# The opening of a one-core decoder layer, in a written order: loads split and regrouped, block 0 first, four weight tiles ahead

## The chip, the cores and the metric

The kernel runs on one core of a Trainium2 chip. A core has five engines, each with its own queue of instructions that it works off in order: TensorE (PE in the profile; PEld is its loading of weights), VectorE (DVE), ScalarE (ACT), GpSimd (POOL) and SyncE (SP), which here only issues transfers between main memory and the on-chip memory. Engines wait for each other through semaphores. The metric is the time of one execution on the device in microseconds (us); lower is better.

## The reference

One layer of a decoder on 256 rows (tokens) of 2048 columns in float32. Nine vectors of 2048 (shift, scale and gate for each of three sub-layers) are made from a conditioning vector c; then come a SwiGLU network, a pair of token mixers (retention and windowed attention) side by side, a second SwiGLU network and a last norm. Only the first lines matter here:

```python
c_act = silu(c)
mod = (c_act @ w_ada + b_ada).reshape(b, 9, 2048)
h = rms_norm(x, norm_ffn1) * (1 + mod[:, 1]) + mod[:, 0]
gate, up = split(h @ w_ffn1_gu, 2)            # 2048 x 11264
x = x + 0.5 * mod[:, 2] * ((silu(gate) * up) @ w_ffn1_down)
h = rms_norm(x, norm_mix) * (1 + mod[:, 4]) + mod[:, 3]
...
```

So nothing of the first large product can start before silu(c), two rows of 128 columns of `mod` for the block at hand, and the root mean square of the rows of x are known.

## The kernel before

**Products.** The 256 rows are two row tiles t of 128; the 2048 columns are 16 blocks k of 128. A large product keeps full float32 accuracy with three TensorE products: each operand is split into a high part (a cast to the rounded format on ACT) and a low part (a subtraction on DVE), and high x high, low x high and high x low are added in one PSUM bank (`products`, L327 to L329). `split` (L335 on ACT, L336 on DVE) makes the parts of a weight tile; `modulated` (L497 on ACT, L502 on ACT, L503 on DVE) applies shift and scale to a block of x, already turned so that columns lie on partitions, and makes its two parts `held.hi` and `held.lo` (hh and hl in the profile).

**Conditioning.** One row (m, k) of the transposed `w_ada` is a tile of 128 x 2048 (1 MB). DVE multiplies it with silu(c), which stands in all 128 partitions (`cact`), and sums along the row: a *pass* (`ada_pass`, L204), here two passes of 1024 columns a row. `ada_end` (L221 to L224) adds the two sums, the bias and, for a scale, the gain. silu(c) comes from four TensorE products of a row of ones with a quarter of c (L170), which copies c to all partitions, and four ACT operations (L171).

**The first stage.** Twelve column tiles n of `w_ffn1_gu` (512 columns each; even n gates, odd n ups) go through five groups of blocks k: 0 to 1, 2 to 4, 5 to 7, 8 to 11, 12 to 15. In each group `visit` loads one tile for the group's blocks, splits it and adds its products; the sum is moved from PSUM to on-chip memory by `to_parts` (L837, L835) and added to by the next group. While a group runs, a generator `group` works off the rows (1, k) and (0, k) of the next group, one row at a time between the tiles, and then scales (L787), turns (L788) and modulates the blocks. The first group's rows, blocks and both row tiles' norms come ahead of the loop.

**What sets the order.** SP's queue has the order of the code. On the other engines a planner orders instructions by its own estimates, within the dependencies, except where `manual_schedule(engines=ORDERED)` gives the code's own order to PE, DVE and ACT too; before, that is done around the norms between stages, not in the opening. A weight tile waits for one of four `raw` buffers, a split for one of three buffers (`wsp`), a row of conditioning after the first two for one of two ring places. A transfer of SP also waits until the eighth before it has landed.

**The opening's loads.** In SP's order: c; row (1, 0) in halves; the two row tiles of x (L762); the unit matrix, three norm gains and the biases (L151 to L157); rows (0, 0), (1, 1), (0, 1) in halves; then the weight tiles (L808). `columns_in` (L178 to L188) turns gains and biases with PE and copies them with DVE. The squares of x are summed by ACT, eight operations of 512 columns (L462); `inv_rms` (L474 to L488) makes the inverse root, with one ACT root. GpSimd's queue holds the load of the tables and masks (L879) and of the sinks (L880), at the start, and then the gate rows (L281).

## Time and profile before

| | |
|---|---|
| time, median of three runs | 2431.64 us (2431.32 to 2433.16) |
| profiled execution: its span from the first to the last instruction | 2429.6 us |
| PE busy | 2385.2 us (98%) |
| DVE busy | 1701.3 us (70%) |
| ACT busy | 1236.0 us (51%) |
| mean rate of the transfers | 250 GB/s |
| first product of a weight tile (L327) | at 26.57 us |

The time of the profiled execution itself is given only by its span; the three timed runs lie 1.7 to 3.6 us above it.

Rows of the profile are read like this. In a view in order of time: start, duration, engine, line of the kernel, operation, what it writes and reads, how often, and in brackets the idle time of the engine before it with what ended that. In a view of groups: line, engine, operation, tiles, shapes, count, then busy us and the mean of one in ns, then the idle time in front of the group and what ended it. In a view of windows: the stretch, its length, then for each engine busy time and number of instructions, then the granted clock of TensorE, the busy share of the transfer engines and GB/s. In a view of transfers: tiles, issuing queue, count, KB each, and the us from issue to landing. A matmul's duration covers its way through the pipeline; successive ones start closer together.

### The profile page before, as it was taken

What the parts mean: (1) busy time and instruction counts of PE and PEld (TensorE: products, weight loads), DVE (VectorE), ACT (ScalarE), POOL (GpSimd) and SP (SyncE); (2) the same over time, 40 slices, a digit from 0 to 9 for tenths busy, and PEclk for the clock granted to TensorE, in tenths of its full rate; (3) what the DMA queues carried; (4) which work ended last, traced back from release to release, by engine and by line L of the source; (5) the groups of instructions that cost most, each with busy time, mean ns of one, the idle gap of its engine ahead of it and who ended that gap; (6) DMA issues with size and microseconds to landing.
All of it is one profiled execution on the core that took longest, in us unless ns stands there. A gap on an engine that the chain in (4) does not pass through costs nothing. (4 is left out here: it accounts for less than half of the span.)

```text
span 2429.6 us, 29064 instructions
## 1 busy us (share of the span) xinstructions
PE 2385.2 (98%) x10798; PEld 1946.8 (80%) x10798; DVE 1701.3 (70%) x2735; ACT 1236.0 (51%) x1696; POOL 5.7 (0%) x14
## 2 busy tenths in 40 slices
PE   7999999999999999999999999999999999999998
PEld 4778888888787777788888888887788888888886
DVE  6998777778877677886666776767655555555656
ACT  6544545454545455554544444446554555554544
POOL 0000000000000000000000000000000000000000
PEclk9999999999999999999999999999999999999999
DMA  9987689998875665566676777755677777775563
GB/s 347 341 333 284 217 313 318 356 319 295 311 264 186 243 222 204 206 219 216 233 266 245 251 260 260 279 189 190 215 249 237 243 251 238 248 237 192 185 198 122
DMA packets 274545, 606.43 MB, mean 250 GB/s; under 512 B 40098, under 2 KB 40482, under 8 KB 255586
## 3 DMA queue, kind: packets, MB, share of 16 engines
q1 hardware_dynamic: 272898, 597.91, 70.8%
q0 software_dynamic: 928, 5.61, 0.6%
q8 instruction: 85, 1.39, 0.2%
q10 hardware_dynamic: 576, 1.05, 0.1%
q14 instruction: 58, 0.47, 0.1%
HBM read 595.06 MB, written 2.12 MB: 246 GB/s over the span
## 5 line engine op out<-in xcount | busy, mean ns | idle before, releaser
L336 DVE TENSOR_TENSOR wl<-raw,wh 128x1024 fp32r<-128x1024 f32 (+1 forms) x828 | 995.9, 1208 | 591.2 <-ACT wh L335 585.3
L335 ACT CAST wh<-raw 128x1024 fp32r<-128x1024 f32 (+1 forms) x828 | 861.4, 1042 | 973.0 <-PE pa L328 936.8
L327 PE MATMUL pa<-wh,hh 128*128 128x512 f32 x2224 | 870.5, 393 | 3.4 <-ACT wh L335 2.9
L328 PE MATMUL pa<-wh,hl 128*128 128x512 f32 x2224 | 869.9, 391 | 2.2 <-DVE hl L503 1.8
L329 PE MATMUL pa<-wl,hh 128*128 128x512 f32 x2224 | 798.0, 392 | 4.0 <-DVE wl L336 4.0
L327 PEld LDWEIGHTS pa<-wh,hh 128*128 128x128 f32 x2224 | 418.1, 188 | 93.4 <-ACT wh L335 4.4
L329 PEld LDWEIGHTS pa<-wl,hh 128*128 128x128 f32 x2224 | 415.9, 188 | 95.9 <-DVE wl L336 9.8
L328 PEld LDWEIGHTS pa<-wh,hl 128*128 128x128 f32 x2224 | 418.3, 188 | 89.8 <-DVE hl L503 2.5
L328 PE MATMUL pa<-wh,a 128*128 128x512 f32 x992 | 383.9, 389 | 0.0
L327 PE MATMUL pa<-wh,a 128*128 128x512 f32 x992 | 367.1, 390 | 1.6 <-DVE t L546 1.2
L329 PE MATMUL pa<-wl,a 128*128 128x512 f32 x992 | 367.1, 390 | 0.8 <-DVE wl L336 0.8
L327 PEld LDWEIGHTS pa<-wh,a 128*128 128x128 f32 x992 | 186.1, 188 | 41.5 <-DVE t L546 1.9
L329 PEld LDWEIGHTS pa<-wl,a 128*128 128x128 f32 x992 | 185.9, 188 | 40.6 <-DVE wl L336 2.4
L328 PEld LDWEIGHTS pa<-wh,a 128*128 128x128 f32 x992 | 186.3, 188 | 38.5
L204 DVE CUSTOM_DVE_ANT_0 slot<-slot,cact 128x512 f32<-128x512 f32 (+1 forms) x252 | 192.8, 814 | 10.5 <-DMA slot<-in_w_ada_dram 10.3
L204 DVE CUSTOM_DVE_ANT_0 raw<-raw,cact 128x512 f32<-128x512 f32 (+1 forms) x260 | 167.1, 696 | 42.5 <-DMA raw<-in_w_ada_dram 32.3
L368 DVE TENSOR_TENSOR a<-slot,a 128x512 fp32r<-128x512 f32 x124 | 85.0, 686 | 13.2 <-ACT a L367 13.2
L367 ACT CAST a<-slot 128x512 fp32r<-128x512 f32 x124 | 76.4, 616 | 14.8 <-PE pa L329 14.7
L442 ACT COPY slot<-a 128x512 uint16<-128x512 uint16 x54 | 38.5, 772 | 31.3 <-DMA a<-a 31.3
L204 DVE DVE_READ_ACCUMULATOR2_ANT sums<- 128x1 f32 x512 | 42.4, 83 | 0.0
L418 ACT COPY slot<-ps 128x512 f32<-128x512 f32 x52 | 29.4, 584 | 23.7 <-PE ps L417 23.5
L462 ACT ACTIVATE pd<-x_sb 128x512 f32<-128x512 f32 x32 | 19.0, 593 | 34.6 <-DVE x_sb L547 32.1
(164 smaller groups left out, 1024.2 us busy)
## 6 DMA issues: line engine op xcount, KB each, us to landing
raw<-in_w_ffn_gu_dram SPq DMA_DIRECT2D x152, 1024.0 KB, 5.2
raw<-in_w_in_dram SPq DMA_DIRECT2D x104, 1024.0 KB, 5.0
raw<-in_w_ffn_down_dram SPq DMA_DIRECT2D x88, 1024.0 KB, 5.1
slot<-in_w_ada_dram SPq DMA_DIRECT2D x76, 1024.0 KB, 7.3
raw<-in_w_ada_dram SPq DMA_DIRECT2D x64, 1024.0 KB, 4.8
raw<-in_w_ffn_gu_dram SPq DMA_DIRECT2D x24, 768.0 KB, 6.9
raw<-in_w_swa_branch_dram SPq DMA_DIRECT2D x16, 1024.0 KB, 5.3
raw<-in_w_ret_branch_dram SPq DMA_DIRECT2D x16, 1024.0 KB, 5.1
```

What stands on the lines that cost most here:

```text
L204: nc.vector.tensor_tensor_reduce(out=w[:, at], in0=w[:, at], in1=cact[:, at], scale=1.0, scalar=0.0, op0=ALU.mult, op1=ALU.add, accum_out= ...
L327: nc.tensor.matmul(ps, ah[:, j, ts], wh[:, j, :], start=first, stop=False)
L328: nc.tensor.matmul(ps, al[:, j, ts], wh[:, j, :], start=False, stop=False)
L329: nc.tensor.matmul(ps, ah[:, j, ts], wl[:, j, :], start=False, stop=last)
L335: nc.scalar.copy(hi, src)
L336: nc.vector.tensor_sub(lo, src, hi.bitcast(F32))
L367: nc.scalar.copy(hi, v)
L368: nc.vector.tensor_sub(lo, v, hi.bitcast(F32))
L418: nc.any.tensor_copy(dest, ps[:, : n * P])
L442: nc.any.tensor_copy(into[:, :, :, i], turned[:, i])
L462: nc.scalar.activation(side_bank(), src, AF.Square, accum_out=dest)
```

## The change

- **c.** The first quarter of `cact` is loaded as a broadcast by SP, and silu is done in place; TensorE spreads the other three quarters.
- **Small loads.** The unit matrix, gains and biases are issued by GpSimd. The tables and sinks that stood first in its queue are ordered behind the first gate row's load.
- **x in halves.** Each row tile of x comes in two loads; the second tile of x comes behind row (0, 0) and the first weight tile.
- **Order.** From silu(c) to the products of the first two weight tiles, PE, DVE and ACT follow the code. The first row tile's root is worked out first: two of its four squares on ACT, the other half in one DVE operation of 1024 columns (`far_squares`). Block 0 goes through scaling, turning, modulation and its products for the first row tile, then for the second, then block 1 follows. Weight tiles are split one block at a time. `root_table` loads ACT's root table right behind silu.
- **Fillers.** `warm(n)` puts n plain float32 products (128 x 512) into a bank that nobody reads.
- **Weight tiles ahead.** Tiles 0 to 3 of the first group are loaded during the opening, ahead of the next group's rows. The next group's passes and scalings are ordered behind the opening's last split, and in the first group the rows are drawn behind the fourth to the tenth tile instead of the second to the tenth.

```diff
     def small_loads():
-        nc.sync.dma_start(ident, consts[:, C_ID : C_ID + P])
+        nc.gpsimd.dma_start(ident, consts[:, C_ID : C_ID + P])
         for i, src in enumerate((norm_ffn1, norm_mix, norm_ffn2)):
-            nc.sync.dma_start(
+            nc.gpsimd.dma_start(
...
     cact = one.tile([P, D], F32, tag="cact", name="cact")
-    for j in range(D // CH):
-        pt = acc_bank()
-        nc.tensor.matmul(pt, ones, c_row[:, j * CH : (j + 1) * CH], start=True, stop=True)
-        nc.scalar.activation(cact[:, j * CH : (j + 1) * CH], pt, AF.Silu)
+    nc.sync.dma_start(cact[:, :CH], c[:, :CH].broadcast_to([P, CH]))
+    small_loads()
+
+    def activate_c():
+        for j in range(D // CH):
+            at = slice(j * CH, (j + 1) * CH)
+            src = cact[:, at]
+            if j:
+                src = acc_bank()
+                nc.tensor.matmul(src, ones, c_row[:, at], start=True, stop=True)
+            nc.scalar.activation(cact[:, at], src, AF.Silu)
...
     place(1, 0)
-    for t in range(NT):
-        nc.sync.dma_start(x_sb[:, t, :], x[0, t * P : (t + 1) * P, :])
-    small_loads()
+    x_load(0)
     place(0, 0)
+    first_two = [load_blocks(0, groups[0])]
+    x_load(1)
     place(1, 1)
     place(0, 1)
-    columns_in()
+    first_two.append(load_blocks(1, groups[0]))
...
+                with tc.issue_after(last_split[1] if ks[0] == 2 else opened[1]):
+                    for q in range(passes):
+                        ada_pass(k, rows_of[m, k], early[m], q, passes)
...
+    def far_squares(t):
+        far = x_sb[:, t, D // 2 :]
+        nc.vector.tensor_tensor_reduce(
+            out=junk, in0=far, in1=far, scale=1.0, scalar=0.0,
+            op0=ALU.mult, op1=ALU.add, accum_out=ssq[:, t * 4 + 2 : t * 4 + 3],
+        )
+
+    def warm(n):
+        idle = side_bank()
+        for _ in range(n):
+            nc.tensor.matmul(idle, ident, x_sb[:, 0, :CH], start=True, stop=True)
...
-    for _ in group(groups[0]):
-        pass
+    with tc.manual_schedule(engines=ORDERED):
+        activate_c()
+        root_table()
+        for q in range(passes):
+            first_pass(1, 0, q)
+        loaded[2] = load_blocks(2, groups[0])
+        columns_in()
+        first_end(1, 0)
+        near_squares(0)
+        warm(2)
+        far_squares(0)
+        r.append(inv_rms(ssq, 0, 3))
+        ps = bank()
+        first_turn(ps, 0, 0)
+        for q in range(passes):
+            first_pass(0, 0, q)
+        loaded[3] = load_blocks(3, groups[0])
+        first_end(0, 0)
+        w00 = first_split(0, 0)
+        modulated(held, 0, ps[:, T[0]], 0, act=True, ts=T[0])
+        banks[0] = [acc_bank() for _ in range(NT)]
+        first_products(0, 0, 0, w00)
+        warm(3)
+        near_squares(1, 4)
+        first_pass(1, 1, 0)
+        r.append(inv_rms(ssq, 1))
+        first_turn(ps, 0, 1)
+        first_pass(1, 1, 1)
+        modulated(held, 0, ps[:, T[1]], 0, act=True, ts=T[1])
+        first_products(0, 0, 1, w00)
+        ps = bank()
+        for t in range(NT):
+            first_turn(ps, 1, t)
+        warm(3)
+        for q in range(passes):
+            first_pass(0, 1, q)
+        first_end(1, 1)
+        first_end(0, 1)
+        modulated(held, 1, ps[:, :S], 0, act=True)
+        w01 = first_split(0, 1)
+        for t in range(NT):
+            first_products(0, 1, t, w01)
+        banks[1] = [acc_bank() for _ in range(NT)]
+        w1 = [first_split(1, k) for k in range(2)]
+        for k in range(2):
+            for t in range(NT):
+                first_products(1, k, t, w1[k])
+        opened = list(last_split)
...
-            visit(n, ks, load_blocks(n, ks), n not in stay)
+            if g > 0 or n > 1:
+                raw = loaded.pop(n) if g == 0 and n in loaded else load_blocks(n, ks)
+                visit(n, ks, raw, n not in stay)
             last = len(order) - 2
-            for _ in range((i + 1) * due // last - i * due // last if i < last else i == last):
+            if g == 0:
+                now = max(0, i - 1) * due // (last - 2) - max(0, i - 2) * due // (last - 2)
+            else:
+                now = (i + 1) * due // last - i * due // last
+            for _ in range(now if i < last else i == last):
                 next(coming, None)
...
-    nc.gpsimd.dma_start(small_c[:, C_COS:], consts[:, C_COS:C_DEC])
-    nc.gpsimd.dma_start(sink_b, sinks.broadcast_to([P, QH]))
+    with tc.issue_after(gate_loaded.ins):
+        nc.gpsimd.dma_start(small_c[:, C_COS:], consts[:, C_COS:C_DEC])
+        nc.gpsimd.dma_start(sink_b, sinks.broadcast_to([P, QH]))
```

More of the change, by code (lines that the diff above doesn't have):

```diff
@@ L280, in gate_load @@
     def gate_load(row, m):
-        nc.gpsimd.dma_start(row, gate_d[m // 3][None, :].broadcast_to([P, D]))
+        return nc.gpsimd.dma_start(row, gate_d[m // 3][None, :].broadcast_to([P, D]))
     pace = {"steps": iter(()), "rate": 0.0, "due": 0.0, "behind": None}
@@ new lines, in layer_kernel, with first_pass, first_end, near_squares @@
+    ssq = small(NT * 4, "ssq")
+    r = []
+    junk = part[2][:, 3 * NT * CH :]
+    def first_pass(m, k, q):
+        ada_pass(k, rows_of[m, k], early[m], q, passes)
+    def first_end(m, k):
+        ada_end(m, slice(k, k + 1), early[m], 0 if m else None, passes)
+    def near_squares(t, n=2):
+        for ci in range(n):
+            square_sum(
+                ssq[:, t * 4 + ci : t * 4 + ci + 1], x_sb[:, t, ci * CH : (ci + 1) * CH]
+            )
+    def far_squares(t):
+        far = x_sb[:, t, D // 2 :]
+        nc.vector.tensor_tensor_reduce(
+            out=junk,
+            in0=far,
+            in1=far,
+            scale=1.0,
+            scalar=0.0,
+            op0=ALU.mult,
+            op1=ALU.add,
+            accum_out=ssq[:, t * 4 + 2 : t * 4 + 3],
+        )
@@ L814, in visit, with first_split @@
+    def first_split(n, k):
+        return split(wsp, "w", first_two[n][:, k : k + 1, :], CH)
+    banks, moved = {}, set()
+    chunks = list(range(2 * EARLY))
     def visit(n, ks, raw, ends, step=2):
```

100 lines of the change are left out of this document (54 added, 46 removed).

## The prediction, made before the changed kernel was run

> **What bounds the kernel now.** I read the page first, then windows up to 226 us, then the order of time in the opening, then the groups by form, then the DMA issues.
>
> ```profile
> span 2429.6 us, 29064 instructions
> PE 2385.2 (98%) x10798; PEld 1946.8 (80%) x10798; DVE 1701.3 (70%) x2735; ACT 1236.0 (51%) x1696; POOL 5.7 (0%) x14
> ```
>
> TensorE (PE) bounds the whole, and only the opening and the stage behind it leave it idle. The windows (us of the stretch, then busy time and count of PE, PEld, DVE, ACT, POOL, then clock, DMA share, GB/s):
>
> ```profile
> 12.00:32.32 20.32, 8.43 (x22) 5.81 (x23) 16.56 (x48) 13.14 (x31) 0.00 (x0) 1.00 0.99 367
> 32.32:58.52 26.20, 25.09 (x109) 19.78 (x107) 21.58 (x34) 18.29 (x28) 0.00 (x0) 1.00 1.00 370
> 58.52:160.00 101.48, 97.24 (x418) 76.03 (x418) 94.16 (x146) 49.18 (x75) 0.00 (x0) 1.00 0.87 324
> 160.00:226.00 66.00, 65.59 (x293) 53.93 (x293) 62.48 (x95) 32.27 (x45) 0.00 (x0) 1.00 0.93 347
> 26.57:32.20 5.63, 5.63 (x14) 4.43 (x15) 4.85 (x6) 3.30 (x6) 0.00 (x0) 1.00 1.03 406
> 32.67:39.00 6.33, 6.33 (x29) 5.25 (x28) 4.39 (x6) 4.63 (x8) 0.00 (x0) 1.00 1.02 397
> ```
>
> Until 32 us PE does little. From 32 to 160 us it is nearly full, but VectorE (DVE) is nearly full too: 94.16 of 101.48 us. DVE splits every weight tile and works off the conditioning rows, so a product cannot pass it. The end therefore moves by as much as DVE's queue moves up to 160 us; a PE that starts early and then meets a late DVE gives the lead back. I measure the lead at two points of that queue: the split of the third weight tile (32.32 before) and that of the eleventh (58.52 before).
>
> The opening in order of time (start, us, engine, line, operation, in brackets the idle time before it):
>
> ```profile
> 1.26 0.68 POOL L879 DMA_DIRECT2D small_c<-in_consts_dram  x1 [0.81 <-POOLq L1229]
> 1.93 0.54 POOL L880 DMA_DIRECT2D sink_b<-in_sinks_dram  x1
> 2.60 7.16 PE L170 MATMUL pa<-c_row,t 1*128 1x512 f32 x8 [2.60 <-DMA c_row<-in_c_dram]
> 8.09 0.60 ACT L171 ACTIVATE cact<-pa 128x512 f32<-128x512 f32 x1 [1.11 <-PE pa L170]
> 11.18 0.60 ACT L462 ACTIVATE pd<-x_sb 128x512 f32<-128x512 f32 x1 [2.49 <-DMA x_sb<-in_x_dram]
> 11.81 0.58 ACT L171 ACTIVATE cact<-pa 128x512 f32<-128x512 f32 x1
> 12.42 1.22 DVE L204 CUSTOM_DVE_ANT_0 raw<-raw,cact 128x1024 f32<-128x1024 f32 x1 [4.17 <-ACT cact L171]
> 12.90 0.59 ACT L462 ACTIVATE pd<-x_sb 128x512 f32<-128x512 f32 x1
> 13.51 0.58 ACT L462 ACTIVATE pd<-x_sb 128x512 f32<-128x512 f32 x1
> 14.86 0.34 PE L178 MATMUL ps<-small_c,t 48*128 48x48 f32 x1 [5.10 <-DMA t<-in_norm_ffn_dram]
> 15.46 1.28 ACT L477 ACT_TABLE_LOAD   x1
> 15.86 0.21 DVE L185 COPY gains<-ps 128x48 f32<-128x48 f32 x1 [1.26 <-PE ps L180]
> 16.76 0.29 ACT L477 ACTIVATE rs<-sum,eps 128x1 f32<-128x1 f32 x1
> 17.09 0.16 DVE L481 RECIPROCAL rs<-rs 128x1 f32<-128x1 f32 x1 [0.44 <-ACT rs L477]
> 20.09 0.40 ACT L787 ACTIVATE t<-x_sb,rs 128x128 f32<-128x128 f32 x1 [0.92 <-DVE rs L488]
> 26.57 0.80 PE L327 MATMUL pa<-wh,hh 128*128 128x512 f32 x1 [0.81 <-ACT wh L335]
> 30.03 1.22 DVE L204 CUSTOM_DVE_ANT_0 slot<-slot,cact 128x1024 f32<-128x1024 f32 x1
> 31.18 1.22 DVE L204 CUSTOM_DVE_ANT_0 slot<-slot,cact 128x1024 f32<-128x1024 f32 x1
> 32.32 1.22 DVE L336 TENSOR_TENSOR wl<-raw,wh 128x1024 fp32r<-128x1024 f32 x1
> ```
>
> Two waits stand out. The last quarter of silu(c) ran at 11.81, because ScalarE (ACT) stood in front of a square that waited for x, and DVE's second pass waited for it until 12.42. The gains and biases came to DVE at 15.86, because they are the last of SyncE's small loads. A pass costs DVE 1.15 (30.03 to 31.18), so a row of two passes costs 2.3.
>
> **The change, part by part.** Durations of one, from the groups by form:
>
> ```profile
> L336 DVE TENSOR_TENSOR wl<-raw,wh 128x512 fp32r<-128x512 f32 x24 | 16.5, 688 | 2.3 <-ACT wh L335 1.6 <-PE pa L329 0.7
> L335 ACT CAST wh<-raw 128x1024 fp32r<-128x1024 f32 x84 | 88.3, 1053 | 75.8 <-PE pa L328 70.8 <-DMA raw<-in_w_ffn_gu_dram 1.9 <-issue 1.6
> L335 ACT CAST wh<-raw 128x512 fp32r<-128x512 f32 x24 | 14.9, 623 | 39.1 <-PE pa L328 39.1
> L837 ACT COPY slot<-pa 128x512 f32<-128x512 f32 x24 | 13.7, 593 | 9.3 <-PE pa L329 8.8
> L497 ACT ACTIVATE t<-ps,modc 128x256 f32<-128x256 f32 x16 | 9.0, 564 | 6.0 <-PE ps L788 5.9
> L503 DVE TENSOR_TENSOR hl<-t,hh 128x256 fp32r<-128x256 f32 x16 | 6.6, 421 | 1.8 <-ACT hh L502 1.5
> L502 ACT CAST hh<-t 128x256 fp32r<-128x256 f32 x16 | 6.3, 395 | 0.0
> ```
>
> *Loads.* SyncE's queue loses six small issues and gains the broadcast quarter of c (256 KB), two more x issues and earlier weight tiles. Taking c's arrival (2.60) and 406 GB/s, I get by bytes: row (1,0) at 5.8 (1.25 MiB ahead and with it, 3.2 us), x's first tile at 8.4, row (0,0) at 11.0, x's second tile at 14.9, row (0,1) at 20.0, four weight tiles by 24. All come before the walk below asks for them; an earlier x alone gains nothing more.
>
> *c.* PE does three quarters instead of four, with the same pace (7.16 us for eight passes), so its third result is again there at 8.09 and silu ends at 8.7. The loaded quarter is hidden behind PE's first. DVE's second pass starts at 8.7 instead of 12.42: 3.7 us gained, ending at 9.9.
>
> *Small loads on GpSimd (POOL).* The rows for that queue:
>
> ```profile
> small_c<-in_consts_dram POOLq DMA_DIRECT2D x1, 320.0 KB, 5.1
> gate_d<-t POOLq DMA_DIRECT2D x3, 8.0 KB, 3.1
> sink_b<-in_sinks_dram POOLq DMA_DIRECT2D x1, 16.0 KB, 7.3
> ```
>
> Six issues at about 0.6 put the last at 4.3. If each lands on its own, 3.1 to 5.1 later, the last is there at 7.4 to 9.4. If they follow each other as the two of before did (6.4, then 9.2: 2.9 apart), at 21. All six are small, nearest to the 3.1 row; I take 8.4. Three transposes (1.0) make it 9.4, just hidden behind the pass that ends at 9.9. The two loads of tables and sinks that leave this place now stand in GpSimd's queue behind the load of the first gate row; only a later stage reads them, so I cost them at nothing. If that cover were gone, DVE would wait for them there.
>
> *First row tile.* ACT loads the root table (1.28 and 0.29) from 8.7 to 10.3, then two squares at 0.61 to 11.5. DVE: copies, biases and the three steps of the scale, 1.3, to 11.2; the added square over 1024 columns, one pass, to 12.4; the root's chain (0.29 and six steps at 0.16) to 13.75. Row (0,0), 2.3, and two short steps end at 16.5. On ACT the modulation and cast of a half width (0.40 and an estimated 0.3, between nothing and the 0.395 of the whole) end at 17.3. The first product starts at 17.4 instead of 26.57.
>
> *Second row tile.* That lead of 9 us is not kept. ACT, in its order, does four squares from 17.3 to 19.8; the root's chain gives r at 21.1, the scaled x at 21.6. PE however has three products and three fp32 fillers (six passes) before that transpose. At the pace of c's matmuls (0.855 a pass) they end at 23.8. Before, PE's pace rose from 14 matmuls in 5.63 us to 29 in 6.33, 5.6 us after its steady work began; so I let it rise at 17.4 + 5.6 = 23.0, and the fillers end at 23.4. The transpose waits 1.8 us for them, with ACT and DVE behind it. Transpose, modulation, cast and low part then end at 25.0.
>
> A rule bears on this: the Trainium skill, TensorE: Matmul & The Clock Gate, "The HAM clock gate", says that the array runs at half clock until one free-running window of about 3.4 us was busy throughout. The 5.6 us agree with it, c's 7.16 us at one pace do not, if rows of one partition count as busy. By the rule's earliest case the fillers end at 22.3, and the sum below would be 1.1 us better.
>
> *Second k.* Row (0,1), 2.3, and the ends of both rows, 0.75, to 28.1. ACT modulates and casts (0.564, 0.395) to 29.1. DVE does the low part (0.42) and three half splits (0.69, 0.61 apart) to 31.5. ACT has three casts (0.62) to 30.95, two scalings of the next group to 31.6, a copy out (0.593) to 32.2, and only then the third tile's cast (1.05): 33.2. The third split starts at 33.2 instead of 32.32: 0.9 late, though PE has done both first tiles.
>
> *From there to the eleventh tile.* Before, DVE had worked off row (1,2) by 32.32 (30.03 and 31.18). The new clauses order the next group's passes and scalings behind the opening's last split (they add no wait, only places in DVE's and ACT's order), and the first two tiles draw no pass at all; so row (1,2) now comes after the third and fourth splits, 2.3 more for this stretch: 21.6 + 2.3 = 23.9. What it has to put that in is the idle time of the stretch:
>
> ```profile
> L336 DVE TENSOR_TENSOR wl<-raw,wh 128x1024 fp32r<-128x1024 f32 x8 | 9.8, 1224 | 4.2 <-ACT wh L335 4.2
> ```
>
> DVE waited there for ACT, which waited for PE to free a buffer. A DVE that lags does not wait; I leave 0.7 for the cast of the fourth tile and one late row load (between 0 and the old 26.20 less 21.58, 4.6). So 33.2 + 23.9 + 0.7 = 57.8 against 58.52: 0.7 us early. Behind it the order of work is the old one, and I carry 0.7 through.
>
> *The sum.* 2429.6 - 0.7 = 2428.9 of span. The runs' median, 2431.6, lies 2.0 above the profiled span (the runs shown, 2431.3 to 2433.2), which I leave as it is: 2430.9 us. I call changes within 0.2% (4.9 us) no change; that is about what a measurement of this kernel can tell.
>
> **The rivals.**
>
> *The lead is kept (faster).* If PE runs at full pace when the first product comes, the second transpose does not wait, and the third split starts at 31.4; if DVE then never waits to the eleventh, that one starts at 31.4 + 23.9 = 55.3, 3.2 early. Behind it DVE still had waits:
>
> ```profile
> L204 DVE CUSTOM_DVE_ANT_0 slot<-slot,cact 128x1024 f32<-128x1024 f32 x28 | 33.1, 1221 | 1.9 <-DMA slot<-in_w_ada_dram 1.9
> L336 DVE TENSOR_TENSOR wl<-raw,wh 128x1024 fp32r<-128x1024 f32 x24 | 29.3, 1222 | 3.0 <-ACT wh L335 2.9
> ```
>
> With the weight tiles ahead, up to 4.9 us of these could close: 8.1 us in all, 2423.5. For it: DMA share is 1.00 up to 58.52, so fuller early queues help. Against: DVE lags more, not less, when the third tile comes.
>
> *GpSimd's loads come late (slower).* PE's transposes of the columns, and behind them DVE's copies and its whole queue, wait for all six. Each microsecond beyond 8.9 moves everything by one. At 21 that is 12 us, less the 3 to 4 us of waits that close: 2439. It decides (slower by 0.2%) from a landing at about 15. For it: the 7.3 of a 16 KB load. Against: that one was a broadcast in rows of 128 bytes behind 320 KB. The Trainium skill, DMA: Bandwidth & Descriptors, "Anatomy of one DMA — SWDGE (gpsimd) path", counts about 2.0 us fixed for each such transfer; one after the other, the six would land at about 13.6, and the time would be about 2435.
>
> **How the numbers follow.** No change within 0.2%: 0.54 (forecast, with its own range of 2427 to 2434 from the bounds of filler, cast and late row). Faster by over 0.2%: 0.27. Slower by over 0.2%: 0.19, mostly the late loads. For 8 in 10, I cut the outer part of each: 2424.5 to 2437.
>
> **What would show it.** Right: silu's last quarter ends near 8.7; first product near 17.4; the second row tile's transpose ends a PE run of fillers, not a wait for ACT; third split within a microsecond or so of 33, eleventh near 57.8, DVE idle between them under 2 us. Wrong: PE waiting for a software load after 10 us; a third split before 30 us; or a second wait for row loads on DVE between 35 and 60 us.

## The result, and the profile after

The changed kernel takes 2436.79 us (median of 15 runs, 2434.77 to 2438.96), the kernel before 2431.58 us (15 runs, 2430.88 to 2433.16). The ratio is 1.002, with a 95% interval from 1.0014 to 1.0027: 5.2 us or 0.21% slower. The forecast was 2430.9 us, no change, with a range of its own of 2427 to 2434.

The first lines of the page after, and its windows (the columns are those of the prediction's windows). The first two stretches end at the third and at the eleventh weight tile's split, as the prediction's two points do:

```profile
span 2434.6 us, 29113 instructions
PE 2395.7 (98%) x10812; PEld 1949.1 (80%) x10812; DVE 1704.1 (70%) x2740; ACT 1234.5 (51%) x1697; POOL 8.7 (0%) x20
```

```profile
12.00:32.94 20.94, 16.32 (x39) 7.79 (x38) 14.39 (x40) 11.49 (x29) 0.00 (x0) 1.00 0.88 333
32.94:61.10 28.16, 24.85 (x105) 18.89 (x103) 24.11 (x36) 17.55 (x27) 0.00 (x0) 1.00 0.95 360
600.00:640.00 40.00, 40.00 (x178) 33.08 (x177) 33.58 (x62) 18.60 (x23) 0.00 (x0) 1.00 0.88 325
640.00:690.00 50.00, 47.29 (x199) 37.87 (x198) 41.88 (x75) 24.84 (x34) 0.00 (x0) 0.97 0.75 274
```

The last stretch in the kernel before:

```profile
640.00:690.00 50.00, 48.40 (x212) 39.20 (x211) 42.72 (x75) 25.29 (x34) 0.00 (x0) 1.00 0.86 316
```

Two things are to be seen. The stretch from the third to the eleventh split took 28.16 us; VectorE was busy for 24.11 of them and idle for 4.05. And far from the changed code, between 640 and 690 us, TensorE did 199 matmuls where it did 212 before. Thirteen matmuls at 0.225 us (40.00 us by 178, in the window from 600 us, where TensorE never stops) are 2.9 us.

To see where the time goes, I paired ScalarE's instructions of two profiles in order and took the median difference of their start times in a stretch. Against before, the changed kernel is 1.4 us late at 160 to 180 us, 2.4 at 600 to 640, 5.4 at 690 to 740, and 5.4 at its end. So 2.4 us come from the opening and what follows from it, 3.0 from 640 to 690 us, and nothing is added after that. A second profile of the same kernel (e1 below) gives 3.4 and 2.7, so each part is known to about 1 us.

The opening and the stretch behind it in order of time:

```profile
8.07 0.60 ACT L178 ACTIVATE cact<-pa 128x512 f32<-128x512 f32 x1 [0.69 <-PE pa L177]
...
9.01 1.23 DVE L212 CUSTOM_DVE_ANT_0 raw<-raw,cact 128x1024 f32<-128x1024 f32 x1
...
10.61 0.21 DVE L193 COPY gains<-ps 128x48 f32<-128x48 f32 x1 [0.37 <-PE ps L188]
...
18.02 0.79 PE L335 MATMUL pa<-wh,hh 128*128 128x512 f32 x1 [2.65 <-ACT hh L512]
...
19.46 4.51 PE L854 MATMUL pd<-x_sb,small_c 128*128 128x512 f32 x6
...
23.37 0.34 SPq L207 DMA_DIRECT2D slot<-in_w_ada_dram  x1
...
23.81 0.27 PE L849 MATMUL ps<-small_c,t 128*128 128x128 f32 x1
...
28.33 0.56 ACT L507 ACTIVATE t<-ps,modc 128x256 f32<-128x256 f32 x1 [2.83 <-DVE modc L230]
...
30.60 0.37 SPq L778 DMA_DIRECT2D raw<-in_w_ffn_gu_dram  x1
...
31.02 0.46 SPq L207 DMA_DIRECT2D slot<-in_w_ada_dram  x1
...
31.80 0.37 SPq L778 DMA_DIRECT2D raw<-in_w_ffn_gu_dram  x1
...
32.94 1.23 DVE L343 TENSOR_TENSOR wl<-raw,wh 128x1024 fp32r<-128x1024 f32 x1 [1.17 <-ACT wh L343]
...
36.66 1.22 DVE L212 CUSTOM_DVE_ANT_0 slot<-slot,cact 128x1024 f32<-128x1024 f32 x1
...
37.92 0.34 SPq L207 DMA_DIRECT2D slot<-in_w_ada_dram  x1
...
38.35 0.90 SPq L778 DMA_DIRECT2D raw<-in_w_ffn_gu_dram  x2
...
45.96 1.04 ACT L343 CAST wh<-raw 128x1024 fp32r<-128x1024 f32 x1 [2.33 <-DMA raw<-in_w_ffn_gu_dram]
...
47.04 1.22 DVE L343 TENSOR_TENSOR wl<-raw,wh 128x1024 fp32r<-128x1024 f32 x1 [1.79 <-ACT wh L343]
...
56.80 1.23 DVE L343 TENSOR_TENSOR wl<-raw,wh 128x1024 fp32r<-128x1024 f32 x1 [0.87 <-ACT wh L343]
```

Up to the third split the kernel went as forecast (32.94 us, forecast 33.2). Then SyncE issued one row at 23.37 us and nothing until 30.60: the next in its queue was the fifth weight tile, whose buffer was held by the first tile until that tile's second block was split. Behind it came the next row, at 31.02, and the sixth tile, at 31.80. Then SyncE issued nothing again until 37.92: the next row needed the ring place of a row whose last pass VectorE ended at 36.66 + 1.22 = 37.88. The seventh tile stood behind that row, at 38.35; ScalarE, which cast it at 45.96 us, had waited 2.33 us for it, and VectorE then 1.79 us at 47.04.

### The profile page after: what moved, and what is told of

Read it like the earlier page. It is cut to its first block, busy times and chain, and to the rows that moved or that the text cites. A ratio compares the mean times of both kernels' runs of the same rounds, so it can differ in the third digit from the quotient of the medians.

```text
span 2434.6 us, 29113 instructions
## 1 busy us (share of the span) xinstructions
PE 2395.7 (98%) x10812; PEld 1949.1 (80%) x10812; DVE 1704.1 (70%) x2740; ACT 1234.5 (51%) x1697; POOL 8.7 (0%) x20
```

## The experiments

No run leaves out a part of the computation; nobody reads what the fillers write. Each time stands beside a run of the kernel before on the same chip (2431.55 to 2431.64 us, the median of each set of runs). In every table "shift" is the median difference against the first profile of before, in us, as above.

### First group: again, and three edits of the opening

The changed kernel again:

> The changed kernel, unchanged, a second time. The first profile of it loses time in two places against before: 2.1 to 2.6 us between the third and the eleventh weight tile's split (28.16 us there, 26.20 before), and 3.2 us more at 653 to 661 us, where a TensorE gap of 2.42 us is followed by a granted clock of 0.50 for some 4 us. Theory (both belong to the program): the same two places again, a stretch of 28 us, a gap of over 2 us near 655 us with a halved clock behind it, a time of 2436 to 2438. Rival (the second place was chance in one execution): no halved clock near 655 us, the shift at the end like that at 600 us, about 2.2 us, and the profiled execution at 2432 to 2434.

The first weight tile split whole:

```diff
-        w00 = first_split(0, 0)
+        w0 = split(wsp, "w", first_two[0][:, :2], CH)
+        w00, w01 = [tuple(p[:, k : k + 1, :] for p in w0) for k in range(2)]
...
-        w01 = first_split(0, 1)
```

> The first weight tile is split in one step of both blocks, where its first block was split, so its buffer is free some 14 us earlier and the fifth tile's load need not wait for it (issued at 30.60 us in the changed kernel, behind nothing on SyncE since 23.8). Theory (the first loop was starved of loads): the fifth tile is issued near 24, VectorE's waits of 1.79 and 0.87 us for casts of late tiles go, the stretch from the third to the eleventh split falls from 28.16 to about 25.5 us, and at 100 us the kernel stands level with before or ahead. Rival (the stretch is long because row (1, 2) was moved into it, 2.3 us of VectorE's work): it stays at 28 us whatever the loads do. Time by the theory 2434 if the second loss (3.2 us near 655 us) stays, 2431 if it goes with it; by the rival 2436.5 or 2433.5.

The rows drawn as before:

```diff
-            if g == 0:
-                now = max(0, i - 1) * due // (last - 2) - max(0, i - 2) * due // (last - 2)
-            else:
-                now = (i + 1) * due // last - i * due // last
+            now = (i + 1) * due // last - i * due // last
```

> The rows of the next group are drawn in the first loop as before: behind the second to the tenth tile, not behind the fourth to the tenth. Theory (starved loads): the fifth tile's load still waits for the first tile's buffer until about 30.6, so the eleventh split stays within 0.7 us of 61.10; row (1, 2) only changes sides, the third split 2.3 us later and the stretch 2.3 us shorter. Rival (the place of the row is the loss): the eleventh split comes 1.5 to 2.5 us earlier, near 59. Time by the theory within 1 us of the changed kernel, less 3.2 if the second loss goes; by the rival some 2 us less.

The fillers ahead of the second transpose left out:

```diff
-        warm(3)
         near_squares(1, 4)
```

> The three float32 fillers between the first row tile's products and the second row tile's transpose are left out. Theory (they hold the second transpose back, which started at 23.81 behind fillers that ran until then at 0.75 us a pass): the transpose at 22.0 to 22.4, the third split 1.2 to 1.6 us earlier than 32.94, the fifth tile's load too, and the eleventh split about 1.4 earlier. Rival (they are needed to raise the pace): the transpose comes earlier, but the products until 28 us run at half pace, and the third split stays within 0.5 of 32.94. Time by the theory 2435.4, by the rival 2436.8, each 3.2 less if the second loss goes.

| run | time, us (range) | ratio, 95% | third split | eleventh | shift 160-180 | 600-640 | 690-740 |
|---|---|---|---|---|---|---|---|
| changed | 2436.79 (2434.77-2438.96) | 1.0014-1.0027 | 32.94 | 61.10 | 1.4 | 2.4 | 5.4 |
| e1, again | 2436.79 (2435.49-2438.41) | 1.0012-1.0029 | 32.34 | 60.63 | 1.2 | 3.4 | 6.1 |
| e2, split whole | 2434.40 (2431.82-2436.23) | 1.0001-1.0018 | 31.54 | 59.32 | -0.4 | 1.1 | 3.3 |
| e3, rows as before | 2433.47 (2430.82-2435.03) | 0.9997-1.0015 | 33.60 | 57.42 | -2.1 | -0.5 | 3.2 |
| e4, three fillers less | 2432.45 (2430.66-2436.15) | 0.9994-1.0013 | 31.72 | 59.48 | 0.2 | 0.0 | 0.1 |

The loss repeats (e1), in both places, though without the halved clock that its theory also forecast (the second group comes back to it). In e2 the fifth tile's load moved from 30.60 to 23.89 us and filled the hole in SyncE's queue, but the stretch stayed at 27.78 us, not 25.5: my theory that one held buffer starves the loop fell. In e3 the stretch was 23.82 us and the eleventh split 3.7 us earlier, so the rival won: the place of the rows is the loss (2.5 us less work and 1.8 less idle time in the stretch, its start 0.7 later). The windows of that stretch in e3:

```profile
33.60:57.42 23.82, 22.90 (x100) 18.31 (x98) 21.58 (x35) 16.62 (x26) 0.00 (x0) 1.00 0.98 372
```

VectorE's 21.58 us of work are those of before in the same stretch, but its idle time is 2.2 us, not 4.6 (before) or 4.05 (changed). The mechanism is in the order of time, in SyncE's and VectorE's rows of e3 (first fence) and of e2 (second):

```profile
23.72 3.79 SPq L207 DMA_DIRECT2D slot<-in_w_ada_dram  x2
30.22 0.38 SPq L778 DMA_DIRECT2D raw<-in_w_ffn_gu_dram  x1
```

```profile
26.66 0.34 SPq L207 DMA_DIRECT2D slot<-in_w_ada_dram  x1
...
30.32 0.37 SPq L778 DMA_DIRECT2D raw<-in_w_ffn_gu_dram  x1
...
35.25 1.22 DVE L212 CUSTOM_DVE_ANT_0 slot<-slot,cact 128x1024 f32<-128x1024 f32 x1
...
36.51 0.34 SPq L207 DMA_DIRECT2D slot<-in_w_ada_dram  x1
```

With rows drawn early (e3) two rows are issued into the hole and the fifth tile behind them. With rows drawn late (e2) SyncE issues nothing from 30.69 to 36.51 us: the next row needs the ring place of row (1, 2), and VectorE passes that row only behind the fourth split, until 35.25 + 1.22 = 36.47 us. The weight tiles queue behind that row. The changed kernel has the same hole, from 31.80 + 0.37 = 32.17 to 37.92 us; in before it ends at 32.43. That it is the ring place is read from these times (0.04 us apart in both), not tried by itself.

e4 gives what the three fillers cost: the second transpose started at 22.39 us instead of 23.81 and the third split came 1.2 us earlier, as its theory said. The eleventh came 1.6 us earlier.

Between 640 and 690 us e2 and e3 lose another 2.2 and 3.7 us, and e4 loses nothing.

### Second group: what happens at 650 us

One difference beside the opening was a transfer of 16 KB of instructions (1.0 to 1.1 us on one of the transfer engines) in the middle of a weight load. (A "gap" of TensorE at this place runs from the start of the last product before it to the start of the next; in brackets the profile shows the idle time within it, 0.4 us less.) Eight products of one column in the opening of the kernel before move it:

```diff
             visit(n, ks, load_blocks(n, ks), n not in stay)
+            if g == 1 and i in (2, 6):
+                idle = side_bank()
+                for _ in range(4):
+                    nc.tensor.matmul(idle[:, :1], ident, ident[:, :1], start=True, stop=True)
```

> The kernel before, with eight products of one column (128 x 1) put into TensorE's queue in the opening, where TensorE is idle until 26.57 us; no other instruction changes its place on TensorE, VectorE or ScalarE. What this changes is how far TensorE's program is when the clock shows a given time, and so when its next 16 KB of instructions are fetched: one fetch came at 648.63 us before, at the end of the loads issued at 639.0 to 642.5, and at 647.60 in the changed kernel, 2.7 us behind the issue of the last of them and in the middle of its transfer, which took 8.2 us there and 6.7 before. Theory (the second loss comes from that fetch): the fetch at 645 to 647 us, the load of 642.54 landing 1 to 1.6 us later than 649.21, the TensorE gap of 1.60 us at 651.3 grows to 2.1 or more, and the kernel loses 1 to 4 us there, 2433 to 2435. Rival (the loss comes from the changed kernel's own order or its shift in time): the gap stays at 1.60 us and the time within 0.7 us of before, 2431 to 2432.3.

e6 is the changed kernel with no fillers:

```diff
-        warm(2)
...
-        warm(3)
...
-        warm(3)
```

> The changed kernel without any of its eight fillers. Its order behind 658 us stays that of the changed kernel (the kernel without only the first three has the order of before there), while TensorE's program is shorter by as much as that of the kernel before is. Theory (the second loss comes from the moment of TensorE's instruction fetch): no loss at 650 us, the gap 1.6 us, a time of 2431 to 2432.5, as without the first three fillers. Rival (it comes from the planner's order behind it): the gap of over 2 us and the halved clock come back, 2434.5 to 2436. For the opening: the products until 28 us at half pace if fillers alone raise the pace; the third split between 31.5 and 33.

e7 is e2, e3 and e4 together:

> Three edits of the changed kernel together: rows drawn as before, the first weight tile split whole, no fillers ahead of the second transpose. If the gains of the opening add up (3.4 us at the eleventh split for the rows, 1.1 to 1.3 each for the two others, together less where they fill the same hole), the eleventh split comes near 56 us, 2.5 us ahead of before's 58.52, and the kernel is 2 to 3 us ahead at 600 us. The time is then 2428.5 to 2429.5 if the second loss does not come, 2432 if it does.

e8 is e3 without the six fillers behind the first product:

```diff
-        warm(3)
         near_squares(1, 4)
...
-        warm(3)
         for q in range(passes):
```

> The changed kernel with rows drawn as before and without the six fillers behind the first product; the two ahead of it stay. Theory (the rows' place and the fillers are the two losses of the opening): eleventh split near 56.3 us, 2 us ahead of before at 600 us; 2429 to 2430 without the second loss, 2432.5 with it. Rival (the fillers behind the first row tile are needed to hold the pace): products at half pace between 24 and 31 us, the eleventh split at 57.5 or later.

| run | time, us (range) | ratio, 95% | eleventh split | shift 160-180 | 600-640 | 690-740 |
|---|---|---|---|---|---|---|
| e5 | 2432.44 (2431.23-2434.64) | 0.9994-1.0012 | 58.04 | -1.5 | -0.6 | 0.0 |
| e6 | 2436.67 (2435.07-2437.84) | 1.0012-1.0030 | 60.70 | 2.8 | 2.6 | 5.0 |
| e7 | 2428.51 (2427.39-2430.30) | 0.9977-0.9995 | 55.81 | -3.5 | -3.5 | -2.0 |
| e8 | 2432.43 (2430.96-2435.33) | 0.9993-1.0011 | 56.38 | -1.7 | -1.3 | 2.9 |

In e5 the fetch moved as forecast (from 648.63 to 644.41 us, 2.45 us behind the issue of a load that then took 7.93 us, not 6.67), and TensorE's gap at 651 us grew from 1.60 to 2.13. But the loss there was 0.6 us and the time within its uncertainty of before's. In e6 the fetch came at the end of the load (6.2 us behind the issue), the gap was 1.59, and 2.4 us were lost all the same. So the fetch alone is not the cause of the 3 us. The rival of e6, the planner's order, is the nearer with its 2434.5 to 2436 (measured 2436.67); its gap of over 2 us did not come. e7 came at the lower end of what was expected of it and is the first version faster than both kernels; e8 came at its theory's time with the second loss (2432.5).

What made the gap longer is a late row of conditioning. VectorE's pass at this place in before, in e5 and in the changed kernel:

```profile
647.40 0.68 DVE L204 CUSTOM_DVE_ANT_0 slot<-slot,cact 128x512 f32<-128x512 f32 x1
```

```profile
647.34 0.69 DVE L204 CUSTOM_DVE_ANT_0 slot<-slot,cact 128x512 f32<-128x512 f32 x1 [0.44 <-DMA slot<-in_w_ada_dram]
```

```profile
650.61 0.69 DVE L212 CUSTOM_DVE_ANT_0 slot<-slot,cact 128x512 f32<-128x512 f32 x1 [0.73 <-DMA slot<-in_w_ada_dram]
```

In e5 that row's load (issued at 638.86, landed at 647.32) took 8.46 us, not 7.11 as in before. VectorE empties the PSUM banks for TensorE's next products behind these passes, so the gap grows by what VectorE waits (0.5 us in e5, 0.8 in the changed kernel). Of the 17 profiles without held steps (the third group), six show this wait, 0.4 to 1.3 us, and a gap of 2.1 to 3.0 us: the changed kernel, e1, e2, e3, e5 and e14. In all six the fetch came 2.4 to 3.2 us behind the issue of the last weight load. The eleven others have a gap of 1.6 us, two of them (e13 and e17) with a fetch 3.5 us behind it.

### Third group: a repair that was none

In the first half of the first down product, no row step is drawn during its last two weight blocks:

```diff
-        while pace["due"] >= 1.0:
+        while pace["due"] >= 1.0 and not pace.get("hold"):
...
-        banks = gemm(act, w, [0, CH], KT=KT)
+        banks = [[acc_bank() for _ in range(NT)] for _ in range(2)]
+        for kb in range(KT // KB):
+            pace["hold"] = kb >= KT // KB - 2
+            gemm_part(act, w, [0, CH], banks, kb, KT)
+            step()
...
+        pace["hold"] = False
```

> The changed kernel, and in the first half of the first down product no step of the conditioning is drawn while its last two weight blocks are worked off; the steps follow behind. So VectorE empties the four PSUM banks for TensorE's next products before it works on a row, which is the wait behind the TensorE gap near 654 us. The opening is untouched. Theory (3 us of the loss are that gap and the halved clock behind it, some 2 us the opening): the gap falls under 1.2 us, no halved clock behind it, the shift against before stays near 2.2 us up to 600 us and is 1 to 2 us at the end, 2433 to 2434. Rival (the 3 us belong to the shift itself, or to loads that come late whatever VectorE does): 2436 to 2437, a stall of like size near the same place.

> The same edit of the conditioning's steps in the kernel before. Its gap at 651 us was 1.60 us with no halved clock behind it in the profiled execution. Theory (the place costs the kernel before only its gap): 0.5 to 1.2 us faster, 2430.4 to 2431.1. Rival (the kernel before often pays for a halved clock there too): 2 us or more faster, 2429.6 or less.

> Rows drawn as before, the first weight tile split whole, no fillers ahead of the second transpose (2428.51 us, 3.4 us ahead of before at 600 us and 1.3 at its end, after 2.1 lost at 650 to 660 us), and the same edit of the conditioning's steps. Theory: the lead of 3.4 us reaches the end and the gap's own 0.5 to 1 comes on top, 2426.5 to 2427.8. Rival (the loss only moves to another place): 2428 to 2429.

> The kernel before, a second profile. Theory (when the fetch of TensorE's instructions falls is a property of the program): the fetch 6 us or more behind the issue of the last load at 642.5 us, the load 6.6 to 7.2 us long, the gap 1.6 us. Rival (it is chance): another place of the fetch, a load of 8 us, a gap of over 2 us.

Measured: e9 2436.42 us (1.0015 to 1.0034), e10 2434.33 (1.0003 to 1.0020), e11 2431.13 (0.9991 to 1.0008). All three theories missed; e9 came out as its rival, e10 and e11 are 2.8 and 2.6 us slower than the same kernel without the edit. The held steps came out together afterwards, two rows ahead of two weight tiles in SyncE's queue, the second of which landed 10.6 us after its issue in e9 (644.65 to 655.27), and the gap in front of TensorE's next products was 2.37 us in all three (1.6 in before and in e7, 2.42 in the changed kernel). The edit made a wait of its own, so it tells nothing of the cause. e12, before again, gave the first profile's picture: a fetch 6.5 us behind the issue, a load of 7.38 us, a gap of 1.60, the three shifts of the tables within 0.2 us.

### Fourth group: the order at 660 us

Behind the gap the kernels stand in one of two orders. In before's, VectorE does two splits in a row and then the four passes of the next row of conditioning (VectorE's rows alone):

```profile
661.77 2.36 DVE L336 TENSOR_TENSOR wl<-raw,wh 128x1024 fp32r<-128x1024 f32 x2
664.04 0.69 DVE L368 TENSOR_TENSOR a<-slot,a 128x512 fp32r<-128x512 f32 x1
664.64 0.69 DVE L204 CUSTOM_DVE_ANT_0 slot<-slot,cact 128x512 f32<-128x512 f32 x1
```

In the changed kernel's, the passes stand in front of the second of these splits, and the row has not landed (rows of VectorE, the last one of TensorE):

```profile
665.23 1.23 DVE L343 TENSOR_TENSOR wl<-raw,wh 128x1024 fp32r<-128x1024 f32 x1 [0.23 <-ACT wh L343]
667.23 0.69 DVE L212 CUSTOM_DVE_ANT_0 slot<-slot,cact 128x512 f32<-128x512 f32 x1 [0.77 <-DMA slot<-in_w_ada_dram]
...
669.68 1.22 DVE L343 TENSOR_TENSOR wl<-raw,wh 128x1024 fp32r<-128x1024 f32 x1
...
670.96 0.73 PE L337 MATMUL pa<-wl,a 128*128 128x512 f32 x2 [0.28 <-DVE wl L343]
```

Nothing in that code was changed. The planner works with its own clock, and the new opening moves what stands on it; a choice 630 us later fell the other way. One filler more or less in the opening is enough to turn it, which gives pairs of kernels that hardly differ otherwise.

e13 has before's order, e14 the changed kernel's. Both are the changed kernel with fewer fillers behind the second row tile's products, one and two; e13's edit is

```diff
-        warm(3)
+        warm(1)
         for q in range(passes):
             first_pass(0, 1, q)
```

e15, with before's order, is e7 without the first two fillers; e16, with the changed kernel's, is e7 with the edit just shown:

```diff
         near_squares(0)
-        warm(2)
         far_squares(0)
```

> The changed kernel with one filler instead of three behind the second row tile's products, where TensorE waits for the next block anyway. With it the planner's order at 658 us is that of the kernel before (a weight tile's second split ahead of the row's passes); with two fillers it is the changed kernel's. The opening and the moment of the fetch move by less than a microsecond. Theory (the order costs 2 us or more there): no wait of VectorE for a row near 667 us ahead of a split, and 2434 to 2435.5. Rival (fetch and halved clock are the whole): the gap of over 2 us stays, and the time within 0.6 us of 2436.8.

> The same with two fillers instead of three: the planner's order at 658 us stays the changed kernel's. Theory (order): VectorE waits about 1 us for a row near 667 us ahead of a split, and TensorE for that split or with a halved clock; 2436.3 to 2437. Rival (fetch and clock): as with one filler, within 0.6 us of it.

> The three edits of 2428.51 us (rows as before, first tile split whole, no fillers ahead of the second transpose), and the two fillers ahead of the first transpose left out too; at 658 us the order of before. If these two fillers do nothing but fill TensorE's idle time, 2428 to 2429, the first product at the same time; if they raise the pace of what follows, the eleventh split comes 0.5 us or more later.

> The three edits, and one filler instead of three behind the second row tile's products; at 658 us this gives the changed kernel's order. Theory (order): 1.5 to 3 us more than 2428.51, with VectorE's wait for a row near 660 us ahead of a split. Rival (order is worth nothing): 2428 to 2429.

The last two runs have before's order too. e17 is the changed kernel with this edit, and e18 is e7 with `warm(2)` in place of the other `warm(3)`, the one ahead of row (0, 1)'s passes:

```diff
-        warm(3)
+        warm(2)
         near_squares(1, 4)
```

> The changed kernel with two fillers instead of three ahead of the second transpose; the three behind the second row tile's products stay. At 658 us the order is that of before. Theory (the order is worth about 2 us, a filler in that place 0.5 to 0.8): VectorE does not wait for a row ahead of a split between 655 and 670 us, the loss between 640 and 700 us is under 1.4 us, or under 3 with a halved clock, and the median is 2433.3 to 2434.5. Rival (the order is worth nothing): 2436 or more.

> The three edits with two fillers instead of three behind the second row tile's products, and the order of before at 658 us. If the opening is as good as with one filler (4.3 us ahead at 119 us) and nothing is lost at 660 us: 2427 to 2428. If it is as with three: 2428.5.

| run, order at 660 us | time, us (range) | ratio, 95% | shift 160-180 | 600-640 | 690-740 |
|---|---|---|---|---|---|
| e13, before's | 2434.30 (2431.63-2436.80) | 1.0000-1.0018 | 3.5 | 3.8 | 3.8 |
| e14, changed | 2436.40 (2433.96-2438.09) | 1.0009-1.0026 | 0.9 | 1.5 | 4.7 |
| e15, before's | 2428.88 (2427.84-2430.36) | 0.9979-0.9996 | -2.6 | -2.8 | -2.7 |
| e16, changed | 2429.12 (2428.46-2431.27) | 0.9980-0.9998 | -4.7 | -4.7 | -2.6 |
| e17, before's | 2433.03 (2431.94-2438.42) | 0.9998-1.0016 | 0.4 | 0.9 | 0.9 |
| e18, before's | 2427.91 (2427.19-2430.15) | 0.9975-0.9992 | -4.5 | -4.5 | -4.4 |

With the new order e16 lost 2.1 us there and e14 3.2; with the old one the four others lost 0.1 or less. e16 shows the wait by itself, with the clock at 1.00 and the fetch out of the way. VectorE's and TensorE's rows in order of time:

```profile
656.90 1.23 DVE L343 TENSOR_TENSOR wl<-raw,wh 128x1024 fp32r<-128x1024 f32 x1
...
659.13 0.69 DVE L212 CUSTOM_DVE_ANT_0 slot<-slot,cact 128x512 f32<-128x512 f32 x1 [1.00 <-DMA slot<-in_w_ada_dram]
...
660.49 0.61 PE L335 MATMUL pa<-wh,a 128*128 128x512 f32 x2
...
661.59 1.22 DVE L343 TENSOR_TENSOR wl<-raw,wh 128x1024 fp32r<-128x1024 f32 x1
...
662.86 0.73 PE L337 MATMUL pa<-wl,a 128*128 128x512 f32 x2 [1.76 <-DVE wl L343]
```

VectorE waits 1.00 us for the row, then passes it for 2.46 us, and TensorE waits for the split behind it. e16's time missed its expectation (0.6 us above e7, not 1.5 to 3, and only 0.24 above e15): its opening was some 2 us better than e15's, and the order cost it 2.1.

The pair e13 and e14 is blurred by another thing. With one filler, TensorE was idle for 2.81 us ahead of block 1 in e13's profile, and its clock fell:

```profile
28.00:30.00 2.00, 0.00 (x0) 0.00 (x0) 0.90 (x7) 0.86 (x2) 0.00 (x0) 1.00 0.39 160
30.00:32.00 2.00, 1.32 (x4) 0.80 (x4) 1.77 (x4) 2.00 (x6) 0.00 (x0) 0.81 0.00 0
32.00:36.00 4.00, 4.00 (x15) 3.11 (x14) 1.77 (x2) 2.98 (x5) 0.00 (x0) 0.67 0.91 307
```

That profiled run took 2435.55 us; the fastest of the same kernel 2431.63. e17 keeps those fillers: 2433.03 us, 0.3 us below the range that its theory gave, against 2436.79 with the changed kernel's order. By the shifts of the two profiles, 1.5 us of the 4.5 between them come before 640 us and 3.0 from 640 to 690.

The windows 640 to 690 us of all kernels without held steps put two of the causes side by side (count of matmuls; the clock granted in that window):

| order at 660 us | clock 1.00 | clock 0.93 to 0.97 |
|---|---|---|
| before's | before 212, e4 212, e5 210, e13 212, e15 212, e17 212, e18 212 | e7 206, e2 202, e3 197 |
| changed | e1 200, e16 203 | changed 199, e6 202, e14 198, e8 194 |

In e16, where the gap is 1.6 us, the order costs 9 matmuls (2.0 us) with no loss of clock; in e1, the changed kernel itself, 12 are lost with no loss of clock, 2 of them by the longer gap (2.07 us). With the old order 6 to 15 are lost where the clock fell, with the new one 10 to 18. The causes do not add up. The changed kernel's profile has the clock at half for 3.41 us behind its gap:

```profile
657.90:661.31 3.41, 3.41 (x8) 2.73 (x9) 3.41 (x5) 0.76 (x3) 0.00 (x0) 0.50 0.75 250
```

Of its 13 matmuls about 7 went there (8 done, where 15 fit at 0.225 us), about 4 in the longer gap and only 2 at the late split, which TensorE, late already, reached 0.28 us before it was there (the row at 670.96). In e1 the clock did not fall, and TensorE waited 1.93 us for that split. So the changed order alone is enough for some 2 us, a late row with a fallen clock behind it for 2 to 4 (e2 2.2 and e3 3.7, with the old order), and the changed kernel had both; neither of them came in before, e4, e13, e15, e17 and e18, which lost 0.1 us or less.

Whether the new order makes the clock fall oftener: in e8 it fell at 668 us, behind a wait of 2.21 us for the late split. In the six others it fell at the gap, ahead of the place where the orders part: 3 of the 11 profiles with the old order (e12 counted) and 3 of the 6 with the new. That is too few to tell.

e18's rows at that place, and its third to eleventh split:

```profile
657.22 2.36 DVE L343 TENSOR_TENSOR wl<-raw,wh 128x1024 fp32r<-128x1024 f32 x2
...
660.10 0.68 DVE L212 CUSTOM_DVE_ANT_0 slot<-slot,cact 128x512 f32<-128x512 f32 x1
```

```profile
32.08:55.24 23.16, 23.11 (x101) 18.54 (x100) 21.59 (x34) 16.34 (x25) 0.00 (x0) 1.00 1.00 378
```

TensorE is busy for 23.11 of 23.16 us there and the transfers all the time. e18 is 3.6 us faster than before and 8.9 faster than the changed kernel.

## Why the prediction was wrong

**The opening, up to the third split: right.** Silu's last quarter ended at 8.67 us (forecast 8.7), the first product started at 18.02 (forecast 17.4, though its own terms add up to about 16.9), the second transpose behind the fillers at 23.81 (23.4), the third split at 32.94 (33.2). Inside it, two terms were off and hidden: the loads came up to 3 us later than by bytes (x's second tile at 18.07 us, forecast 14.9), and GpSimd's last small load at 10.16 us (forecast 8.4, at most 9.4), which cost VectorE 0.37 us at 10.61. Neither rival came in: the lead was not kept, and GpSimd's loads stayed 4.8 us short of the point from which they decide.

**The stretch to the eleventh split: wrong, and one term of it.** "A DVE that lags does not wait; I leave 0.7." VectorE's work was 24.11 us (forecast 23.9), its idle time 4.05 (forecast 0.7). The step took the waits of before for slack that the moved row would fill, and it read them as waits for a buffer. The row of before says otherwise: ScalarE waits in front of its copies, for TensorE's sums, and the casts stand behind the copies.

```profile
L837 ACT COPY slot<-pa 128x512 f32<-128x512 f32 x20 | 11.5, 592 | 8.5 <-PE pa L329 8.0
```

Beside that, SyncE's queue is in order: a row that is drawn late frees its ring place late, and then not only rows but the weight tiles behind them come late. In the changed kernel ScalarE waited 3.2 us for such tiles in this stretch, in e3 0.3. e3 shows the price of that place: 3.7 us at the eleventh split. VectorE's idle time is still 2.2 us there, so about 1.8 of the 3.35 us that the term missed come from the rows' place and 1.5 are waits for casts that the term had left out anyway. Of the bounds that I gave, 0 and 4.6, the upper one was the nearer.

**"Behind it the order of work is the old one, and I carry 0.7 through": wrong.** Up to 600 us 2.4 us stood, and 3.0 more were lost between 640 and 690 us, more than half of the whole loss, in code that the change does not touch. The order of VectorE's work at 660 us was not the old one; by itself that cost 2.1 us in e16. In the changed kernel's own profile most of the 3.0 went to the longer gap and the half clock behind it, and in e1, the same program, most went to the order. The step argued from the code, which is the same there; the order that the planner makes of that code is not, and it is fixed in both programs before either runs. Nor are the times the same at which rows and instructions are fetched.

**The clock.** The Trainium skill, TensorE: Matmul & The Clock Gate, "What's actually happening", says that the array falls to half clock after at least one idle window of about 3.4 us, and that the window is free-running. The second half fits these runs: with the same gap of 1.59 or 1.60 us the clock fell in e6 and e7 (0.97 over the window above) and did not in before, e4, e13, e15, e16, e17 and e18. In the changed kernel the fall lasted 3.41 us, as long as one such window. The first half does not cover them: idle times of 1.21 us (e6 and e7), 2.03 (changed) and, in the opening, 2.81 (e13), as the profile counts them, were enough, and 1.69 (e1) and 1.74 (e5) were not. Behind the longer gaps (2.07 to 2.96 us, e2's and e3's among them) it fell in four profiles of six, behind the gap of 1.6 us in two of eleven. What decides it is open.

## What to carry to other kernels

Where a planner orders the work, compare the whole order of both programs, to the end, and not only where the edit is: one filler in the opening turned a choice 630 us later that was worth some 2 us, and it moved fetches and rows there as well. Where two causes overlap, one profile shows only the one that came first: the second profile of the same kernel (e1) showed the other. Before a stage's idle time is counted as room for moved work, look at what ends each of its waits: in a queue that issues in order, a late row makes the tiles behind it late too. And try the parts of a change one by one: here the opening was worth 4.5 us at 600 us (e18) once its rows were drawn as before, the first tile split whole and four of its eight fillers left out.

## What the runs showed of the hardware

- A fetch of instructions shares the transfer engines with the loads. In 17 profiles (all but those with held steps) the last weight load ahead of the gap took 7.9 to 8.8 us where TensorE's 16 KB of instructions were fetched 2.4 to 3.5 us behind its issue, and 6.7 to 7.4 us where they came 6.0 us or more behind it, when its transfers were nearly over. The packet itself takes 1.0 to 1.1 us, and in the changed kernel the load's last packets ran one behind the other from 651.3 to 652.7 us. Eight small products more in TensorE's queue (e5) were enough to move the fetch into the load. The Trainium skill, Runtime: NRT & Kernel Launch, "Instruction fetch mechanics", calls the crossing of a 16 KiB boundary mostly hidden. No wait of TensorE at this place ends with the fetch; the load beside it came up to 2 us later. The products rarely waited for that load; what cost time was the row of conditioning in flight beside it (8.46 us in e5, 7.11 in before), which VectorE waited for in six profiles.
- The two fillers ahead of the first transpose (3.78 us, all at the slow pace, 0.85 to 1.0 us from start to start) bought nothing: in e15, which has none of them, the first three products took 0.80, 0.66 and 0.63 us, in the changed kernel 0.79, 0.63 and 0.63.
- GpSimd's six small loads landed at 6.17, 7.53, 8.95, 9.34, 9.84 and 10.16 us, 0.3 to 1.4 us apart, neither all alone nor 2.9 us apart.
- The granted clock of the windows does not show the slow pace of the opening. In the changed kernel the passes of the fillers start 0.85 us apart from 19.46 to 22.87 us and 0.43 apart from 26.07 on, and the record says 1.00 for both stretches. In the opening the pace is read from the starts of like instructions.
